# Weight chunks laid out by the host as they lie in SBUF: one run per partition in place of 1 KB pieces

## The chip, the cores and the metric

The kernel runs on one core of a Trainium2 chip. The metric is the device time of one execution in microseconds (us); the times below are of whole executions, the profile is of one execution taken by the hardware profiler. TensorE (PE) does the matmuls, VectorE (DVE) and ScalarE (ACT) the work on elements, GpSimd (POOL) a little at the end of a layer; SyncE (SP) only issues DMAs. The DMA engines copy between the chip's main memory (HBM) and the 128 partitions of the on-chip memory (SBUF).

## The reference

A generator of two layers over 256 latent and 256 context tokens of width 1024. Layer 0 works on all 512 tokens, layer 1 needs an output for the 256 latent ones only. Cut to what matters:

```python
def trunk_layer(x, xc, mod, mod_c, ...):
    sh1, sc1, g1, sh2, sc2, g2 = split(mod, 6)           # mod = silu(c) @ w_ada + b_ada
    h = modulate(rms_norm(x, norm1), sh1, sc1)           # the same for the context: hc
    y, yc = token_mixer(h, hc, ...)
    x = x + g1 * y
    x = x + g2 * moe_ffn(modulate(rms_norm(x, norm2), sh2, sc2), ...)

def token_mixer(h, hc, ...):
    f_in, p_in, qb, kb, vb, qw, kw, vw = split(h @ w_in)
    # a: Fourier mix of f_in, b: global attention, c: window attention, d: pooling of p_in
    return branch_merge(h, (out_a, out_b, out_c, out_d), w_branch, w_gate, b_gate, w_out)

def branch_merge(h, branches, w_branch, w_gate, b_gate, w_out):
    merged = zeros_like(h)
    for i, br in enumerate(branches):
        gate = sigmoid(h @ w_gate[i] + b_gate[i])
        merged = merged + gate * (br @ w_branch[i])
    return merged @ w_out

def moe_ffn(h, router_w, router_bias, w1, w3, w2):       # 16 experts of width 512, 2 per token
    for e in range(N_EXPERTS):
        hid = silu(tok @ w1[e]) * (tok @ w3[e])
        out = out + combine[:, e:e + 1] * (hid @ w2[e])
```

All weights are float32, and nearly all of the time goes with reading them: 2 layers with 16 experts of 6 MB, 24 MB of w_ada, 16 MB of w_gate, 8 MB of w_branch, 4 MB of w_out and some 10 MB of w_in.

## The kernel before

**Weights come in chunks.** A chunk is at most 1 MB and lies in SBUF as 128 partitions of 2048 float32 (CH = 2048, 8 KB). The class `Stream` keeps the chunks in the order of their use, which a dry run of the whole program takes down. `fill` issues loads on SyncE's queue as far as the rings have room: `stage` has four buffers; while the experts run there is also the ring `ext`, and some large tiles (`hH`, `hL`, `X`) serve as buffers when nothing else is in them. `load` issues a chunk's DMA. `emit` (called from `tick` and `get`) splits a chunk into a high and a low float16 part: `whi` on ScalarE (L325) and then `wlo` on VectorE (L329). Three matmuls (`mm3`, L586 to L588) put a product together from the parts: `hH` by `whi`, `hL` by `whi`, `hH` by `wlo`. The chunks of w_ada are used in float32 as they come (L506).

**The kinds of chunks** are in `load`. `cols` (w_in, w_gate, w_out, w1, w3) and `ada` take 256 columns of a matrix of 1024 rows: row p + 128 k goes to partition p, so that a partition gets eight pieces of 1 KB, from eight rows. `half` takes 128 columns, eight pieces of 512 bytes. `rows` takes `n` columns of a matrix of 512 rows, four pieces a partition: 1 KB for w_branch (n = 256), 2 KB for w2 (n = 512, also as `raw`). `q` takes 256 columns out of 512, in two DMAs of 512-byte pieces. `heads` (w_branch of branches b and c) has rows by head and takes two DMAs, one for partitions 0 to 63 and one for 64 to 127, each 256 KB.

**The order of work.** A scheduler sets the order of every engine's instructions ahead of time; each engine then runs its own list in order, and SyncE's list is one queue of DMAs. The transposes of the attention probabilities (`pt` or `pair` from `P`, L778) go through the same queue of SyncE. The tiles of x and ctx, the tables, and the experts' results go through ScalarE's queue.

**The places that matter here.** At the start `ada` (L502 on) turns the conditioning vectors into shifts and scales (`adah`, `adal`, L483 and L484), while ScalarE sums the squares of x (L536). `gated(i)` (L1002 on) runs four steps for each of the four branches; a step takes a w_gate chunk, makes two `gate` tiles on ScalarE (L1019), takes a w_branch chunk and adds the product to `merged`. The `po` matmuls (L846) of attention read the transposed `pt`. Each of 16 experts takes two chunks of w1, two of w3 and two of w2; `sa` (L1393) on ScalarE is reached once an expert, `hd` are its hidden values. In the trace w1, w2 and w3 have one name, `in_w_dram`. During `gated` of branch c the first expert chunks are already being loaded into `ext`.

Of the kernel before, what the change touches and what calls it, by code (L numbers as in the profile page):

```python
# [19 lines left out]
KD = D // 128  # L20
T = 256
NTOK = 512
HD = 64
# [6 lines left out]
WS = 512.0  # L30
# [83 lines left out]
class Dry:  # L114
    """Stands in for the chip while the order of the weight chunks is taken down."""

# [19 lines left out]
class Pool:  # L136
    def __init__(self, pool, bufs):
        self.pool, self.bufs = pool, bufs
# [6 lines left out]
def k8(t):  # L145
    return t.rearrange("p (k c) -> p k c", k=KD)


def k4(t):
    return t.rearrange("p (k c) -> p k c", k=4)  # L150


class Stream:
    """Weight chunks in the order of their use: DMAs run ahead as far as staging space goes, and
    each chunk's fp16 high and low parts are made up to `look` chunks ahead."""

# [38 lines left out]
    def load(self, spec, st):  # L195
        A, sp = self.kn.A, self.kn.nc.sync
        if self.behind:
            self.kn.tc.keep_in_program_order(self.kn.nc.vector.memset(st.rearrange("p (k c) -> p k c", c=128)[:, :, 0:1], 0.0))
        kind, name, idx, c0 = spec[:4]
        w = A[name]  # L200
        for i in idx:
            w = w[i]
        if kind == "half":
            sp.dma_start(k8(st[:, 0:1024]), w[:, c0:c0 + 128].rearrange("(k p) c -> p k c", p=128))
        elif kind in ("cols", "ada"):
            sp.dma_start(k8(st), w[:, c0:c0 + 256].rearrange("(k p) c -> p k c", p=128))
        elif kind == "q":
            src = w[:, c0:c0 + 512].rearrange("(k p) (a c) -> p k a c", p=128, a=2)[:, :, :, spec[4] * 128:spec[4] * 128 + 128]
            view = st.rearrange("p (k a c) -> p k a c", k=KD, a=2)
            for a in range(2):  # L210
                sp.dma_start(view[:, :, a, :], src[:, :, a, :])
        elif kind in ("rows", "raw"):
            n = spec[4]
            sp.dma_start(k4(st[:, 0:4 * n]), w[:, c0:c0 + n].rearrange("(k p) c -> p k c", p=128))
        else:
            n = spec[4]
            src = w[:, c0:c0 + n].rearrange("(a j d) n -> a d j n", a=2, j=4)
            for a in range(2):
                sp.dma_start(k4(st[a * HD:(a + 1) * HD, 0:4 * n]), src[a])

# [17 lines left out]
    def emit(self, j):  # L238
        spec, st = self.order[j], self.stage[j]
        if self.piece == 0:  # L240
            pool = self.kn.wsp
            if self.kn.ext is not None and spec[1] in ("w1", "w2", "w3"):
                self.parts += 1
                if self.parts % (NWSP + self.kn.more) < self.kn.more:
                    pool = self.kn.ext
            self.tiles[j] = tuple(pool.tile([128, CH], F16, name=n) for n in ("whi", "wlo"))
        hi, lo = self.tiles[j]
        if spec[0] == "q":
            u = self.piece
            d = lambda t: t.rearrange("p (k u a d) -> p k u a d", k=KD, u=2, a=2)[:, :, u]  # L250
            src = st.rearrange("p (k a u d) -> p k a u d", k=KD, a=2, u=2)[:, :, :, u]
            self.kn.split(d(hi), d(lo), src, WS)
            done = u == 1
        else:
            n = 1024 if spec[0] == "half" else 4 * spec[4] if spec[0] in ("rows", "heads") else CH
            step = CH if spec[1] in ("w1", "w2", "w3") else 1024
            s = slice(self.piece * step, min(n, (self.piece + 1) * step))
            self.kn.split(hi[:, s], lo[:, s], st[:, s], WS)
            done = (self.piece + 1) * step >= n
        self.piece += 1  # L260
        if done:
            self.piece = 0
            self.split += 1
            self.stage.pop(j)
# [50 lines left out]
class Kernel:  # L315
    def __init__(self, tc, A, out, orders, dry=False):
        self.tc, self.A, self.out, self.orders, self.dry = tc, A, out, orders, dry
        self.nc = tc.nc
        self.ext = None
        self.h_free = False  # L320
        self.pin = False
# [17 lines left out]

# [1 line left out]
    def setup(self, ctx):  # L341
# [48 lines left out]
    def table_load(self, lo, hi):  # L390
        """Part of the staged constants, asked for once the vector engine has come this far."""
        st = self.wk.tile([128, 512], F32, "tabs", tag="t2")
        self.after(self.nc.vector.memset(st[:, 0:1], 0.0))
        self.nc.scalar.dma_start(st[:, 0:hi - lo], self.A["staged"][:, lo:hi])
        return st
# [70 lines left out]

# [1 line left out]
    def ada(self, l, which, tick=True):  # L468
# [63 lines left out]

# [1 line left out]
    def x_stat(self, t, part, lo, n):  # L534
# [54 lines left out]

# [1 line left out]
    def layer(self, l):  # L591
# [492 lines left out]

# [1 line left out]
    def moe(self, l, nt, side):  # L1086
# [172 lines left out]
        def experts(W, hot0, h2):  # L1259
# [35 lines left out]
            def slot_side(e):  # L1295
                """The weights of the expert's slots and its one-hot turned to slots by tokens."""
                g, el = divmod(e, EPG)
# [132 lines left out]
            def side_rows():  # L1430
                """Room and rows that the end needs, once the last group is dispatched."""
                m = self.lay.tile([128, KD, nt], F32, "merged").rearrange("p k c -> p (k c)")
# [92 lines left out]

_RAW = ["x", "ctx", "w_ada", "w_in", "sink", "pool_w", "w_branch", "w_gate", "w_out",
        "router_w", "router_bias", "w1", "w3", "w2", "norm_f"]


def host_arrays(inputs):  # L1530
    arr = {n: np.ascontiguousarray(inputs[n]) for n in _RAW}
# [7 lines left out]
    feature = np.r_[1:64, 0, 64, 127:64:-1]  # L1539
    w = arr["w_branch"]  # L1540
    order = np.r_[tuple(g * 128 + feature for g in range(4))]
    arr["w_branch"] = np.ascontiguousarray(np.concatenate([w[:, 0:1, order], w[:, 1:]], 1))
    arr["consts"], arr["staged"] = shape_constants()
    return arr


def build(inputs):
    import concourse.bacc as _bacc

    nc = _bacc.Bacc("TRN2", target_bir_lowering=False, num_devices=1)  # L1550
    arrays, A = {}, {}
    for name, a in host_arrays(inputs).items():
        arrays[f"in_{name}_dram"] = a
        A[name] = nc.dram_tensor(f"in_{name}_dram", a.shape, mybir.dt.from_np(a.dtype), kind="ExternalInput").ap()
    out = nc.dram_tensor("out_0_dram", (1, T, D), F32, kind="ExternalOutput").ap()
    orders = {}
    Kernel(Dry(), Dry(), Dry(), orders, dry=True).body()
    with tile.TileContext(nc) as tc:
        Kernel(tc, A, out, orders).body()
    return nc, arrays  # L1560
# [8 lines left out]
```

## Time and profile before

| | us |
|---|---|
| three runs | 1497.1, 1509.64, 1510.03 |
| median | 1509.64 |
| span of the profiled execution | 1507.6 |
| TensorE busy | 1389.0 (92%) |
| VectorE busy | 1122.6 (74%) |
| ScalarE busy | 954.0 (63%) |
| SyncE's DMA queue, time with packets, share of the span | 78.8% |
| TensorE waiting for the first w_ada chunk | 12.06 |
| ScalarE's `whi` waiting for expert chunks, whole run | 25.0 |
| `po` waiting for transposes `pt`, whole run | 11.2 |

The profile of the execution lists no time besides its span, which is 2.0 us below the median of the runs. A busy share is an average over the whole program; stretches differ, so the rows further below are taken by stage. An engine's wait is put down to the event that came last.

### The profile page before, as it was taken

The numbers are of one execution on the slowest core, as the hardware profiler recorded it, in microseconds if no ns is written. First come the engines' busy times: TensorE is split into PE (matmuls) and PEld (weight loads), VectorE is DVE, ScalarE is ACT, GpSimd is POOL, SyncE is SP. The second block draws the span as 40 slices with busy tenths as digits, with TensorE's granted clock in tenths as the row PEclk, the third lists the DMA queues.
The fourth block names the chain that finished last, engine by engine and source line by source line (L and its number), as shares of the span: only waits on it lengthen the run. The fifth ranks groups of instructions, "written<-read, shape, count | busy, mean of one in ns | idle before, by whom it ended". The sixth has DMA issues, their size and how long they took to land. (4 is left out here: it accounts for less than half of the span.)

```text
span 1507.6 us, 33938 instructions
## 1 busy us (share of the span) xinstructions
PE 1389.0 (92%) x14303; PEld 941.7 (62%) x14303; DVE 1122.6 (74%) x2039; ACT 954.0 (63%) x1437; POOL 8.8 (1%) x12
## 2 busy tenths in 40 slices
PE   4999999997999998999999878899798889999995
PEld 2545454443444686777777556687686767777773
DVE  3888548767435576898968778869856788988797
ACT  3767535655223457898887466747645578787783
POOL 0000000000000000000000200000000000000000
PEclk9999999998999999999999989999999999999998
DMA  9759864898696346999999873976989879999980
GB/s 331 227 134 221 226 189 114 197 225 219 202 281 199 128 141 235 337 342 365 366 367 361 284 226 120 227 183 164 224 211 299 293 250 325 359 357 362 351 299 31
DMA packets 403194, 375.83 MB, mean 249 GB/s; under 512 B 91728, under 2 KB 364112, under 8 KB 402768
## 3 DMA queue, kind: packets, MB, share of 16 engines
q1 hardware_dynamic: 393616, 355.24, 78.8%
q10 hardware_dynamic: 8256, 14.05, 2.6%
q0 software_dynamic: 1152, 4.19, 0.8%
q8 instruction: 116, 1.90, 0.5%
q14 instruction: 54, 0.44, 0.1%
HBM read 342.78 MB, written 9.70 MB: 234 GB/s over the span
## 5 line engine op out<-in xcount | busy, mean ns | idle before, releaser
L586 PE MATMUL mm<-hH,whi 128*128 128x96 f16 (+2 forms) x1824 | 400.6, 262 | 6.1 <-ACT gate L1019 5.4
L588 PE MATMUL mm<-hH,wlo 128*128 128x96 f16 (+2 forms) x1824 | 400.1, 262 | 4.4 <-DVE wlo L329 4.4
L587 PE MATMUL mm<-hL,whi 128*128 128x96 f16 (+2 forms) x1824 | 400.3, 262 | 0.0
L329 DVE SCALAR_TENSOR_TENSOR wlo<-stage,whi 128x1024 f16<-128x1024 f32 (+1 forms) x208 | 310.3, 1506 | 112.2 <-ACT whi L325 111.3
L586 PEld LDWEIGHTS <-whi 128*128 128x128 f16 x3104 | 305.3, 98 | 79.4 <-issue 6.0
L588 PEld LDWEIGHTS <-wlo 128*128 128x128 f16 x3104 | 305.2, 98 | 78.9 <-DVE wlo L329 6.7
L587 PEld LDWEIGHTS <-whi 128*128 128x128 f16 x3104 | 305.3, 98 | 77.4 <-issue 5.4
L325 ACT ACTIVATE whi<-stage 128x1024 f16<-128x1024 f32 (+1 forms) x208 | 262.2, 1282 | 124.6 <-PE mm L587 77.4
L329 DVE SCALAR_TENSOR_TENSOR wlo<-ext,whi 128x2048 f16<-128x2048 f32 x116 | 262.7, 2285 | 75.3 <-ACT whi L325 75.3
L325 ACT ACTIVATE whi<-ext 128x2048 f16<-128x2048 f32 x116 | 218.7, 1905 | 52.3 <-DMA ext<-in_w_dram 25.0
L586 PE MATMUL mm<-xg,whi 128*128 128x96 f16 x1024 | 132.5, 206 | 0.0
L588 PE MATMUL mm<-xg,wlo 128*128 128x96 f16 x1024 | 132.5, 206 | 0.0
L587 PE MATMUL mm<-xg,whi 128*128 128x96 f16 x1024 | 132.5, 206 | 0.0
L587 PE MATMUL py<-wlo,hd 128*96 128x512 f16 x224 | 84.9, 379 | 4.3 <-DVE wlo L329 4.2
L588 PE MATMUL py<-whi,hd 128*96 128x512 f16 x224 | 84.7, 381 | 2.8 <-DVE hd L327 2.3
L586 PE MATMUL py<-whi,hd 128*96 128x512 f16 x224 | 85.1, 380 | 1.7 <-ACT hd L325 1.7
L586 PE MATMUL mm<-brH,whi 128*128 128x512 f16 (+1 forms) x256 | 83.5, 326 | 0.0
L587 PE MATMUL mm<-brL,whi 128*128 128x512 f16 (+1 forms) x256 | 83.4, 326 | 0.0
L588 PE MATMUL mm<-brH,wlo 128*128 128x512 f16 (+1 forms) x256 | 83.4, 326 | 0.0
L1277 PE MATMUL mm<-Dg,merged 128*128 128x384 f16 x384 | 75.7, 340 | 5.2 <-ACT hH L1279 2.6
L506 PE MATMUL mm<-stage,cpad 128*32 128x256 f32 x768 | 58.1, 406 | 16.0 <-DMA stage<-in_w_ada_dram 16.0
L830 ACT ACTIVATE P<-E,rl 128x512 f16<-128x512 f32 (+1 forms) x96 | 57.1, 643 | 13.2 <-issue 4.9
(311 smaller groups left out, 2128.4 us busy)
## 6 DMA issues: line engine op xcount, KB each, us to landing
ext<-in_w_dram SPq DMA_DIRECT2D x118, 1024.0 KB, 11.5
stage<-in_w_dram SPq DMA_DIRECT2D x62, 1024.0 KB, 10.2
stage<-in_w_ada_dram SPq DMA_DIRECT2D x48, 1024.0 KB, 6.7
stage<-in_w_gate_dram SPq DMA_DIRECT2D x32, 1024.0 KB, 6.0
stage<-in_w_in_dram SPq DMA_DIRECT2D x24, 512.0 KB, 6.4
stage<-in_w_in_dram SPq DMA_DIRECT2D x8, 1024.0 KB, 7.2
stage<-in_w_branch_dram SPq DMA_DIRECT2D x16, 512.0 KB, 4.5
stage<-in_w_branch_dram SPq DMA_DIRECT2D x32, 256.0 KB, 6.6
```

What stands on the lines that cost most here:

```text
L325: a = nc.scalar.activation(hi, src, AF.Copy, scale=scale)
L329: b = nc.vector.scalar_tensor_tensor(lo, src, scale, hi, op0=ALU.mult, op1=ALU.subtract)
L506: pe.matmul(ps[32 * j:32 * j + 32, :], self.cpad[:, 2 * k:2 * k + 32], st[:, k, :], start=k < 4, stop=k >= 4, tile_position=(0, 32 * j))
L586: pe.matmul(ps, wH(k), xH(k), start=first and k == 0, stop=False)
L587: pe.matmul(ps, wH(k), xL(k), start=False, stop=False)
L588: pe.matmul(ps, wL(k), xH(k), start=False, stop=last and k == nk - 1)
L830: act.activation(pv[:, 0, qt, :], E[qt][:, 0:nk], AF.Copy, scale=r[:, qt:qt + 1])
L1277: pe.matmul(ps[:, 0:SLOTS], h2[n][t][:, cs(k)], Dg[:, t].rearrange("p e c -> p (e c)"), start=t == 0, stop=t == ntt - 1)
```

## The change

The host now cuts every weight chunk out of its matrix and writes it as it will lie in SBUF, [128, 2048] float32, all chunks of one weight stacked in one array: a partition's share is one run of 8 KB (4 KB for `half` and w_branch). To know the chunks, the dry run is made ahead of the host's arrays. `load` is then the same single DMA for every kind, `q` and `heads` included; the eight pieces, the two DMAs of `q` and the two of `heads` are gone. `q` lies so that its two halves, which are split one at a time, are contiguous columns. The number of bytes, the rings and the matmuls are the same.

```diff
+def chunk_width(spec):
+    return 1024 if spec[0] == "half" else 4 * spec[4] if spec[0] in ("rows", "raw", "heads") else CH
+
+
+def chunk_of(spec, w):
+
+    kind, _, idx, c0 = spec[:4]
+    for i in idx:
+        w = w[i]
+    n = {"half": 128, "cols": 256, "ada": 256, "q": 512}.get(kind) or spec[4]
+    w = w[:, c0:c0 + n]
+    if kind == "q":
+        w = w.reshape(KD, 128, 2, 2, 2, HD)[:, :, :, spec[4]]
+        return w.transpose(1, 0, 3, 2, 4).reshape(128, CH)
+    if kind == "heads":
+        return w.reshape(2, 4, HD, n).transpose(0, 2, 1, 3).reshape(128, 4 * n)
+    return w.reshape(-1, 128, n).transpose(1, 0, 2).reshape(128, -1)
...
-        kind, name, idx, c0 = spec[:4]
-        w = A[name]
-        for i in idx:
-            w = w[i]
-        if kind == "half":
-            sp.dma_start(k8(st[:, 0:1024]), w[:, c0:c0 + 128].rearrange("(k p) c -> p k c", p=128))
-        elif kind in ("cols", "ada"):
-            sp.dma_start(k8(st), w[:, c0:c0 + 256].rearrange("(k p) c -> p k c", p=128))
-        elif kind == "q":
-            src = w[:, c0:c0 + 512].rearrange("(k p) (a c) -> p k a c", p=128, a=2)[:, :, :, spec[4] * 128:spec[4] * 128 + 128]
-            view = st.rearrange("p (k a c) -> p k a c", k=KD, a=2)
-            for a in range(2):
-                sp.dma_start(view[:, :, a, :], src[:, :, a, :])
-        elif kind in ("rows", "raw"):
-            n = spec[4]
-            sp.dma_start(k4(st[:, 0:4 * n]), w[:, c0:c0 + n].rearrange("(k p) c -> p k c", p=128))
-        else:
-            n = spec[4]
-            src = w[:, c0:c0 + n].rearrange("(a j d) n -> a d j n", a=2, j=4)
-            for a in range(2):
-                sp.dma_start(k4(st[a * HD:(a + 1) * HD, 0:4 * n]), src[a])
+        n = chunk_width(spec)
+        sp.dma_start(st[:, 0:n], A[spec[1]][self.kn.places[spec[1:]]][:, 0:n])
...
-        if spec[0] == "q":
-            u = self.piece
-            d = lambda t: t.rearrange("p (k u a d) -> p k u a d", k=KD, u=2, a=2)[:, :, u]
-            src = st.rearrange("p (k a u d) -> p k a u d", k=KD, a=2, u=2)[:, :, :, u]
-            self.kn.split(d(hi), d(lo), src, WS)
-            done = u == 1
-        else:
-            n = 1024 if spec[0] == "half" else 4 * spec[4] if spec[0] in ("rows", "heads") else CH
-            step = CH if spec[1] in ("w1", "w2", "w3") else 1024
-            s = slice(self.piece * step, min(n, (self.piece + 1) * step))
-            self.kn.split(hi[:, s], lo[:, s], st[:, s], WS)
-            done = (self.piece + 1) * step >= n
+        n = chunk_width(spec)
+        step = CH if spec[1] in ("w1", "w2", "w3") else 1024
+        s = slice(self.piece * step, min(n, (self.piece + 1) * step))
+        self.kn.split(hi[:, s], lo[:, s], st[:, s], WS)
+        done = (self.piece + 1) * step >= n
...
+    chunks, places = {}, {}
+    for specs in orders.values():
+        for spec in specs:
+            if spec[1:] not in places:
+                at = chunks.setdefault(spec[1], [])
+                places[spec[1:]] = len(at)
+                at.append(chunk_of(spec, w_branch if spec[1] == "w_branch" else np.asarray(inputs[spec[1]])))
+    for name, at in chunks.items():
+        arr[name] = np.stack([np.pad(c, ((0, 0), (0, max(x.shape[1] for x in at) - c.shape[1]))) for c in at])
```

The order of TensorE's and GpSimd's instructions is the same in both kernels. The scheduler, which counts one DMA where there were two, has moved a few rows on the other engines. The largest such place is `gated` of branch c in layer 1. On SyncE's queue it reads, before (`ext` are the experts' chunks that are loaded ahead, `stage` those of the gates and branches, and the numbers tell one buffer from another):

```order
L206 DMA stage_19520<-in_w_gate_dram 128x8x256
L206 DMA ext_20227<-in_w3_dram 128x8x256
L219 DMA stage_19556<-in_w_branch_dram 64x4x256 x2
L206 DMA stage_19619<-in_w_gate_dram 128x8x256
L219 DMA stage_19655<-in_w_branch_dram 64x4x256 x2
L206 DMA ext_20229<-in_w3_dram 128x8x256
L206 DMA stage_19718<-in_w_gate_dram 128x8x256
```

and after:

```order
L219 DMA ext_20203<-in_w3_dram 128x2048
L219 DMA stage_19499<-in_w_gate_dram 128x2048
L219 DMA stage_19535<-in_w_branch_dram 128x1024
L219 DMA ext_20205<-in_w3_dram 128x2048
L219 DMA stage_19597<-in_w_gate_dram 128x2048
L219 DMA stage_19633<-in_w_branch_dram 128x1024
```

The first w3 chunk now stands ahead of a gate chunk that it stood behind, and the second (ext_20229 before, ext_20205 after) ahead of the next gate and branch chunks. On ScalarE the same stretch reads, before (a `gate` is made from the product of the gate's chunk, a `whi` is the high part of a chunk):

```order
L1019 ACTIVATE gate<-mm,hbg 128x256
L325 ACTIVATE whi<-stage 128x1024 x2
L1019 ACTIVATE gate<-mm,hbg 128x256
L325 ACTIVATE whi<-stage 128x1024
L1019 ACTIVATE gate<-mm,hbg 128x256
L325 ACTIVATE whi<-ext 128x2048
L325 ACTIVATE whi<-stage 128x1024 x2
L325 ACTIVATE mH_20051<-merged 128x256
```

and after:

```order
L1013 ACTIVATE gate<-mm,hbg 128x256
L319 ACTIVATE whi<-ext 128x2048
L319 ACTIVATE whi<-stage 128x1024 x2
L1013 ACTIVATE gate<-mm,hbg 128x256
L319 ACTIVATE whi<-stage 128x1024
L1013 ACTIVATE gate<-mm,hbg 128x256
```

The split of that w3 chunk has moved four places up, ahead of two gates and the splits between them. The corresponding split in layer 0 has moved two places up, ahead of one gate and one split, and one transpose in attention of layer 0 has changed places with a gate chunk's load.

## Rows read from the trace of the kernel before

**Rows 1.** The page's parts 1 to 3: busy engines, packets, SyncE's queue (q1).

```profile
PE 1389.0 (92%) x14303; PEld 941.7 (62%) x14303; DVE 1122.6 (74%) x2039; ACT 954.0 (63%) x1437; POOL 8.8 (1%) x12
DMA packets 403194, 375.83 MB, mean 249 GB/s; under 512 B 91728, under 2 KB 364112, under 8 KB 402768
q1 hardware_dynamic: 393616, 355.24, 78.8%
```

**Rows 2.** Windows: us; PE, PEld, DVE, ACT, POOL busy; PE clock, DMA share, GB/s.

```profile
700.00:750.00 50.00, 48.61 (x769) 39.65 (x768) 46.97 (x31) 42.83 (x38) 0.00 (x0) 1.00 1.08 365
800.00:825.00 25.00, 21.24 (x316) 16.58 (x313) 22.19 (x14) 18.40 (x15) 0.00 (x0) 1.00 1.07 358
1300.00:1350.00 50.00, 49.49 (x660) 36.74 (x657) 42.80 (x35) 44.80 (x48) 0.00 (x0) 1.00 1.07 359
```

**Rows 3.** Timeline of ScalarE, experts of layer 0: start, duration, instruction, wait.

```profile
728.14 0.48 ACT L1393 ACTIVATE sa<-mm 128x384 f32<-128x384 f32 x1
741.46 0.47 ACT L1393 ACTIVATE sa<-mm 128x384 f32<-128x384 f32 x1
...
797.74 0.48 ACT L1393 ACTIVATE sa<-mm 128x384 f32<-128x384 f32 x1
814.50 0.49 ACT L1393 ACTIVATE sa<-mm 128x384 f32<-128x384 f32 x1 [0.21 <-ACT whi L325]
823.96 1.91 ACT L325 ACTIVATE whi<-stage 128x2048 f16<-128x2048 f32 x1 [1.33 <-DMA stage<-in_w_dram]
831.44 0.47 ACT L1393 ACTIVATE sa<-mm 128x384 f32<-128x384 f32 x1
```

**Rows 4.** Layer 1, 1100 to 1150: SyncE's and ScalarE's timeline; waits (total, times, longest).

```profile
1124.85 1.17 SPq L206 DMA_DIRECT2D ext<-in_w_dram  x1
1139.86 1.91 ACT L325 ACTIVATE whi<-ext 128x2048 f16<-128x2048 f32 x1 [9.12 <-DMA ext<-in_w_dram]
PE mm L586 <- ACT gate L1019: 5.4, 1, 5.4
```

**Rows 5.** DMA from 1100 to 1150: packets; issues (KB each, us to landing).

```profile
DMA packets 12557, 12.63 MB, mean 253 GB/s; under 512 B 288, under 2 KB 12552, under 8 KB 12552
stage<-in_w_branch_dram SPq DMA_DIRECT2D x8, 256.0 KB, 11.7
```

**Rows 6.** Windows behind two pauses of TensorE, columns as in rows 2.

```profile
1087.00:1096.00 9.00, 8.97 (x62) 6.98 (x62) 0.48 (x1) 0.95 (x2) 0.00 (x0) 0.69 0.35 112
1145.00:1154.00 9.00, 8.71 (x57) 6.80 (x58) 7.62 (x13) 5.10 (x9) 0.00 (x0) 0.69 1.09 318
```

**Rows 7.** Waits of the whole run, and SyncE's timeline around the longest transpose wait.

```profile
PE po L846 <- DMA pt<-P: 11.2, 4, 6.6
ACT whi L325 <- DMA stage<-in_w_gate_dram: 10.5, 8, 2.9
1077.00 1.00 SPq L206 DMA_DIRECT2D stage<-in_w_gate_dram  x1
1079.28 0.37 SPq L214 DMA_DIRECT2D stage<-in_w_branch_dram  x1
```

**Rows 8.** DMA of the start: 11 to 30 us, then 6 to 9.5 with ScalarE's queue (q10).

```profile
DMA packets 6801, 6.59 MB, mean 347 GB/s; under 512 B 421, under 2 KB 6671, under 8 KB 6799
DMA packets 599, 1.40 MB, mean 400 GB/s; under 512 B 32, under 2 KB 332, under 8 KB 599
q10 hardware_dynamic: 299, 1.09, 79.6%
```

**Rows 9.** VectorE's split of expert chunks, by form: count, busy, mean ns, idle before.

```profile
L329 DVE SCALAR_TENSOR_TENSOR wlo<-ext,whi 128x2048 f16<-128x2048 f32 x116 | 262.7, 2285 | 75.3 <-ACT whi L325 75.3
```

**Rows 10.** Timelines at the start: first matmul, last x tile, VectorE's first constant.

```profile
12.06 1.93 PE L506 MATMUL mm<-stage,cpad 128*32 128x256 f32 x16 [12.06 <-DMA stage<-in_w_ada_dram]
11.08 0.63 ACT L536 ACTIVATE junk<-X 128x512 f32<-128x512 f32 x1 [0.46 <-DMA X<-in_ctx_dram]
22.03 0.23 DVE L377 CAST id<-cst 128x128 f16<-128x128 f32 x1 [7.12 <-DMA cst<-in_consts_dram]
```

More of the change, by code (lines that the diff above doesn't have):

```diff
@@ L315, with __init__ @@
 class Kernel:
-    def __init__(self, tc, A, out, orders, dry=False):
+    def __init__(self, tc, A, out, orders, places=None, dry=False):
+        self.places = places if places is not None else Dry()
         self.tc, self.A, self.out, self.orders, self.dry = tc, A, out, orders, dry
@@ L1523, in moe, with host_arrays @@
         self.moe_scope.close()
-_RAW = ["x", "ctx", "w_ada", "w_in", "sink", "pool_w", "w_branch", "w_gate", "w_out",
-        "router_w", "router_bias", "w1", "w3", "w2", "norm_f"]
-def host_arrays(inputs):
+_RAW = ["x", "ctx", "sink", "pool_w", "router_w", "router_bias", "norm_f"]
+def host_arrays(inputs, orders):
     arr = {n: np.ascontiguousarray(inputs[n]) for n in _RAW}
@@ L1539, in host_arrays @@
     feature = np.r_[1:64, 0, 64, 127:64:-1]
-    w = arr["w_branch"]
+    w = np.asarray(inputs["w_branch"])
     order = np.r_[tuple(g * 128 + feature for g in range(4))]
-    arr["w_branch"] = np.ascontiguousarray(np.concatenate([w[:, 0:1, order], w[:, 1:]], 1))
+    w_branch = np.concatenate([w[:, 0:1, order], w[:, 1:]], 1)
     arr["consts"], arr["staged"] = shape_constants()
-    return arr
+    chunks, places = {}, {}
[7 more added lines that the diff above has]
+        arr[name] = np.stack([np.pad(c, ((0, 0), (0, max(x.shape[1] for x in at) - c.shape[1]))) for c in at])
+    return arr, places
 def build(inputs):
@@ L1550, in build @@
     nc = _bacc.Bacc("TRN2", target_bir_lowering=False, num_devices=1)
+    orders = {}
+    Kernel(Dry(), Dry(), Dry(), orders, dry=True).body()
     arrays, A = {}, {}
-    for name, a in host_arrays(inputs).items():
+    arr, places = host_arrays(inputs, orders)
+    for name, a in arr.items():
         arrays[f"in_{name}_dram"] = a
@@ L1555, in build @@
     out = nc.dram_tensor("out_0_dram", (1, T, D), F32, kind="ExternalOutput").ap()
-    orders = {}
-    Kernel(Dry(), Dry(), Dry(), orders, dry=True).body()
     with tile.TileContext(nc) as tc:
-        Kernel(tc, A, out, orders).body()
+        Kernel(tc, A, out, orders, places).body()
     return nc, arrays
```

## The prediction

> **What bounds the kernel now.** I began with the page's totals [rows 1]. TensorE is busy for 1389.0 of 1507.6 us, so all that shorter weight transfers can give lies in the other 118.6 us, less those that are chains between the engines, and in stretches at the lower clock. The queue that SyncE feeds has packets under way for 78.8% of the span; most packets are under 2 KB. So transfers are nearly always running; the question is where the program waits for them. That was read stage by stage.
>
> First the 50 us windows of the experts [rows 2]. In layer 0 from 700 to 750 the transfer engines are never idle, and bring 365 GB/s; still TensorE works 48.61 of 50 us, since the staging rings were full when the experts began. From 800 to 825 it is only 21.24 of 25: the rings have run dry. The pace of the experts says it again [rows 3]: from one `sa` to the next it is 741.46 - 728.14 = 13.32 us while fed, but 16.76 us from 797.74 to 814.50 and 16.94 us from there to 831.44, and in that stretch `whi` waits for its chunk (1.33 us at 823.96). In layer 1, between 1300 and 1350, the transfers run as hard (359 GB/s) but TensorE works 49.49 of 50 us: there nothing is to be won.
>
> Second the sums of waits and the places they point to. The longest stall of TensorE on a chunk after the start is in layer 1's `gated(2)` [rows 4]: a matmul waits 5.4 us for `gate` on ScalarE; ScalarE stood 9.12 us before `whi<-ext` at 1139.86, and that chunk had been issued at 1124.85. In those 50 us the engines move only 253 GB/s [rows 5]: the `heads` pieces go to 64 partitions a time, and a 256 KB transfer takes 11.7 us from issue to landing, behind others of its kind. A pause of TensorE costs twice: the 9 us after it ran at a mean granted clock of 0.69 [rows 6], the lower of the two levels (1.2 and 2.4 GHz) for most of them. Third, transposed attention probabilities travel on the same queue: `po` waits 11.2 us in four places for `pt` [rows 7], the longest 6.6, and the 9 us after that show 0.69 too [rows 6].
>
> **The change, part by part.** The same bytes move, in the same order but for a few swaps, in one piece per partition. I need the rate for large pieces. The nearest rows are of the start [rows 8]. From 11 to 30 us, when nearly all packets are under 2 KB, 347 GB/s; from 6 to 9.5 us, when half of the packets are the 4 KB rows of x and ctx (299 packets with 1.09 MB), 400 GB/s. With every weight packet at 4 or 8 KB I take 400 GB/s; the bounds are the 365 of [rows 2] (no gain) and some 420, an estimate that carries the step from 347 to 400, which came with half of the packets, a little further. A loss is a rival below.
>
> One rule speaks against this change. The row first: 400 GB/s with large pieces, for 3.5 us, against 347 to 365 without [rows 2, 8]. The Trainium skill, "DMA: Bandwidth & Descriptors", section "Where 436 GB/s comes from", says that for transfers between HBM and SBUF the memory's share per core, about 358 GB/s, is what binds; the trace goes above it, if briefly and alone. By the rule the sum below would keep only what is won in layer 1's `gated(2)`.
>
> *Experts of layer 0.* An expert takes six chunks, 6.29 MB: 17.2 us at 365 GB/s, 15.7 us at 400. All 96 chunks of a layer, 100.7 MB, take 275.8 us at 365 and 251.7 at 400. The last of them would be there 24 us earlier, and the dry rings cost only some 7 us (below); so any rate over about 375 GB/s (7 us in 276) is enough, and the exact one doesn't matter. What is late next is VectorE: six `wlo` of 2285 ns [rows 9], with the two steps on `sa` and `hd` about 14.8 us for an expert. If the starved two go at the fed pace, 16.76 + 16.94 - 2 x 13.32 = 7.1 us are won; at VectorE's, 16.76 + 16.94 - 2 x 14.8 = 4.1. I take **5**, as VectorE enters the stretch with some lead.
>
> *Layer 1's gated(2).* The `heads` chunks fill 128 partitions in one DMA. At 350 to 400 GB/s in place of 253, the queue in front of the `ext` chunk is gone sooner: in the 15.0 us from issue to landing it moved 3.8 MB, which take 9.5 us at 400. That is 5.5 us sooner, which alone covers the 5.4 us of stall; besides, SyncE issues this load a slot earlier, ahead of a gate chunk of 1 MB (2.6 us at 400). ScalarE's `whi<-ext` also stands four places earlier in its queue, ahead of two gates, so that if the chunk were still late it would hold up more than before. I take the stall as gone, 5.4 us (bounds 2 and 5.4), and with it the low clock behind it: (1 - 0.69) x 9 = 2.8 us. Together **8.2** (5 to 8.2). In layer 0 the same place has no stall of TensorE, and its moved rows are costed at nothing: by the code each matmul there takes 512 tokens in place of 256, which leaves twice the time.
>
> *Transposes.* Ahead of the worst `pt` lie a gate chunk and a branch chunk, 1.57 MB [rows 7]: 4.3 us at 365 GB/s, 3.9 at 400, so each of the four waits is cut by 0.4 us, 1.6 in all, taken as **2**. The bounds are the longest wait, 6.6 us, with the clock's 2.8 us on top, if the queue is free when the transpose is issued, and 0.
>
> *Gate chunks.* `whi` waits 10.5 us for them in eight places [rows 7]; little of it reaches TensorE, which has matmuls of the gate before. **1** (0 to 3).
>
> *Start.* The first matmul waits 12.06 us for its first chunk, since the x tiles come at the same time over ScalarE's queue; of the 599 packets between 6 and 9.5 us, 299 belong to that queue [rows 8], so the rest, nearly as many, to SyncE's: one for one. If that holds for packets of 8 KB beside 4 KB, the 512 rows of x share with 4.2 MB of weights, not 0.5 MB: the last x tile comes about 9 us later (3.7 MB at 400), at about 20 in place of 11.08 us [rows 10], while the chunks come that much earlier. The square sums then end at about 21.5, just about when VectorE's `id<-cst` (22.03) lets the steps behind it go. **0**, from 3 won (chunks are no longer late after that) to 5 lost (x late).
>
> *The rest.* `q` in one DMA, its split in contiguous halves, SyncE with 24 issues less (8 for `q`, 16 for `heads`): SyncE is no bound, and `q` is split beside matmuls: 0, if the cover goes 1 or 2 us. The swapped rows in attention of layer 0: 0 (-2 to 2).
>
> The sum is 5 + 8.2 + 2 + 1 = 16.2 us off the span of 1507.6, 1491.4. The profile has no time of its own besides this span; the median of the three runs is 2.0 above it, so I forecast **1493**. A change of under 1% (15.1 us) can't well be told from none here; faster by over 1% begins at 1494.5.
>
> **Rivals.**
>
> *The rate does not rise* (365 GB/s stays, what binds is not the piece). For it: three stretches, 700 to 750, 1300 to 1350 and 11 to 30, lie within 347 to 365 although the mix of pieces differs. Against it: the 400 of [rows 8], short as it is. Then the experts, the transposes and the gates keep their times, and only the 64 partitions are mended: 1507.6 - 8.2 + 2 = 1501. The rule quoted above gives this result.
>
> *Every wait on a transfer goes, and the clock stays high.* 7.1 for the experts, 8.2, 9.4 for the transposes, 3 for the gates, 3 at the start: 30.7, so 1507.6 - 30.7 + 2 = 1479. For it: the queue gets faster for all of these at once, and a pause that ends sooner also saves the clock. Against it: most of these waits end on VectorE or ScalarE shortly after, which get no faster.
>
> *Slower: large pieces come at a lower rate.* Each transfer engine now reads 8 KB from one place at a time. The place is the experts of layer 0, which draw all that comes; it decides as soon as the rate falls below 365. At 335, a loss of about the size of the gain that I assume, the 96 chunks need 300.5 us, 24.7 more; layer 1, whose queue is just as full but not waited for, some 12 more; with 8 us won in `gated(2)` that is 1507.6 + 24.7 + 12 - 8 + 2 = 1538. Against it: the rows of x are pieces of 4 KB and came fast.
>
> **How the numbers follow.** The forecast has 0.47: its own range is 1487 to 1500, of which about two thirds (0.30) lie below 1494.5. No rise of the rate 0.26, about 1501. All waits gone 0.20. Slower 0.07. So faster 0.30 + 0.20 = 0.50, same 0.17 + 0.26 = 0.43, slower 0.07. The range runs from 1475, beyond the sum of the upper bounds by some us, to 1508, the end of the second case with 5 us lost at the start and the swapped rows on top; it leaves out the slower rival and the outermost of the others.
>
> **What would show it.** Right: over 375 GB/s in layer 0's experts from 650 on, no fall of TensorE's share in the last 50 us of them, and `sa` to `sa` below 15 us throughout; no stall above 2 us in layer 1's `gated(2)` and a clock of 1.00 behind it; the median landing of `w_branch` near half of what it was. Wrong: the same GB/s at full queues; or a new wait of ScalarE for `ext` ahead of the gates; or x that lands so late that the first norm waits for it beyond 24 us; or a queue that is faster, and the same pace of experts, with VectorE busy all through.

## The result, and the profile after

The changed kernel takes 1484.4 us, median of four runs (1481.73 to 1486.71); the kernel before 1507.36 (1497.1 to 1510.03). The ratio is 0.9856, with a 95% interval of 0.9819 to 0.9893: 16 to 27 us faster. The forecast was 1493 in a range of 1475 to 1508, so the sign and the range held, and the gain between the medians, 23 us, was larger by some 7 us than the sum.

The page of the kernel after, lines of its head and of its parts 1 to 3, which answer to [rows 1]:

```profile
span 1480.0 us, 33882 instructions
PE 1378.1 (93%) x14303; PEld 938.7 (63%) x14303; DVE 1122.7 (76%) x2039; ACT 954.3 (64%) x1437; POOL 8.6 (1%) x12
DMA packets 142713, 375.82 MB, mean 254 GB/s; under 512 B 91344, under 2 KB 93392, under 8 KB 104400
q1 hardware_dynamic: 133136, 355.24, 68.5%
```

The span is 27.6 us shorter, more than the 23 us between the medians: the span of 1507.6 belongs to one of the longer runs of the kernel before, that of 1480.0 to the shortest of the four of the kernel after. TensorE's work is the same; 10.9 us of the difference are busy time (1389.0 to 1378.1, the same matmuls at a higher mean clock) and 16.7 idle time. The same 355.24 MB of SyncE's queue go in a third of the packets, and its packets are under way for 68.5% of a shorter span, not 78.8%. The windows of layer 0's experts (columns as in [rows 2]):

```profile
650.00:700.00 50.00, 48.52 (x656) 36.87 (x653) 45.69 (x27) 44.34 (x46) 0.00 (x0) 1.00 1.01 417
700.00:750.00 50.00, 48.82 (x765) 39.51 (x763) 46.98 (x30) 44.32 (x38) 0.00 (x0) 1.00 1.00 400
800.00:825.00 25.00, 23.27 (x353) 18.44 (x352) 24.53 (x13) 22.04 (x18) 0.00 (x0) 1.00 0.93 382
```

417 and 400 GB/s stand where 365 did, and from 800 to 825 TensorE works 23.27 of 25 us in place of 21.24. The timeline of ScalarE there, which answers to [rows 3], has no wait on a chunk:

```profile
793.79 0.48 ACT L1387 ACTIVATE sa<-mm 128x384 f32<-128x384 f32 x1
807.11 0.47 ACT L1387 ACTIVATE sa<-mm 128x384 f32<-128x384 f32 x1
822.73 0.48 ACT L1387 ACTIVATE sa<-mm 128x384 f32<-128x384 f32 x1
834.42 0.47 ACT L1387 ACTIVATE sa<-mm 128x384 f32<-128x384 f32 x1
```

The steps from `sa` to `sa` are 13.32, 15.62 and 11.69 us; before, the first two were 16.76 and 16.94. VectorE, and TensorE's waits from 804 to 823, show what sets the second step now:

```profile
799.27 11.09 DVE L323 SCALAR_TENSOR_TENSOR wlo<-ext,whi 128x2048 f16<-128x2048 f32 x5
810.28 0.55 DVE L1388 SCALAR_TENSOR_TENSOR sa<-mm,sa 128x384 f32<-128x384 f32 x1
810.75 4.49 DVE L323 SCALAR_TENSOR_TENSOR wlo<-ext,whi 128x2048 f16<-128x2048 f32 x2
815.15 0.55 DVE L321 TENSOR_TENSOR hd<-sa,hd 128x384 f16<-128x384 f32 x1
815.62 4.49 DVE L323 SCALAR_TENSOR_TENSOR wlo<-stage,whi 128x2048 f16<-128x2048 f32 x2
```

```profile
PEld L582 <- DVE hd L321: 2.3, 1, 2.3
PE py L581 <- DVE wlo L323: 1.6, 1, 1.6
```

VectorE works without a pause from 799.27 to 820.11, and TensorE (PEld is its weight load) waits for VectorE's `hd` and `wlo`, no longer for chunks. For layer 1's `gated(2)`, ScalarE's timeline (to [rows 4]), the transfers of 1080 to 1130 (to [rows 5]) and windows (to [rows 6]) follow:

```profile
1107.51 1.91 ACT L319 ACTIVATE whi<-ext 128x2048 f16<-128x2048 f32 x1 [1.38 <-DMA ext<-in_w_dram]
```

```profile
stage<-in_w_branch_dram SPq DMA_DIRECT2D x5, 512.0 KB, 4.5
```

```profile
1080.00:1130.00 50.00, 50.00 (x464) 44.52 (x463) 34.42 (x49) 28.00 (x38) 0.00 (x0) 1.00 0.88 339
1123.00:1132.00 9.00, 9.00 (x85) 8.07 (x83) 6.75 (x13) 5.55 (x9) 0.00 (x0) 1.00 1.01 413
1071.00:1080.00 9.00, 9.00 (x61) 6.92 (x61) 1.02 (x3) 1.36 (x3) 0.00 (x0) 0.67 0.33 118
```

TensorE is busy for all of the 50 us at 339 GB/s, its clock stays at 1.00 behind the place, a branch chunk of 512 KB lands 4.5 us after its issue where 256 KB took 11.7, and ScalarE waits 1.38 us for the chunk, not 9.12. The low clock behind the long wait for a transpose (0.67) is still there.

**Where the time went.** TensorE's list of 14303 matmuls is the same in every kernel of this study but the one with transposes on ScalarE's queue, where it differs in places of the attention; so the same matmul can be found in two traces and its start compared. The table gives, for stretches that end at the matmuls which start at the times of the first row in the kernel before, by how many us each kernel is shorter (-) or longer than that trace; the first two kernels are second profiles of before and after, described with the experiments.

| stretch ends (us) | 40 | 400 | 600 | 860 | 1080 | 1120 | 1160 | 1220 | 1493 |
|---|---|---|---|---|---|---|---|---|---|
| before, again | 0.8 | -0.9 | 2.0 | -0.1 | 0.5 | -0.4 | -2.2 | -3.1 | 0.0 |
| after, again | -1.4 | -2.1 | 0.1 | -7.2 | -0.7 | -0.3 | -8.8 | -3.0 | 0.0 |
| after | -1.9 | -2.3 | 2.1 | -8.9 | -3.7 | -1.2 | -8.8 | -3.1 | 0.0 |
| heads alone | 0.5 | -1.4 | 2.1 | 0.9 | -0.7 | 0.0 | -8.7 | -3.3 | 0.0 |
| experts alone | 0.3 | 1.0 | 0.0 | -9.0 | -1.2 | -0.1 | -8.0 | -1.8 | 0.0 |
| heads by halves | -1.5 | 0.4 | 0.0 | -9.0 | -1.9 | 0.3 | -8.2 | -1.7 | 0.0 |
| heads by columns | -1.9 | -2.2 | 2.0 | -8.6 | -3.9 | -1.0 | -8.8 | -3.3 | 0.0 |
| 1 KB pieces | 1.1 | -1.2 | 0.2 | 6.2 | 0.2 | 0.3 | -8.0 | -2.0 | 0.0 |
| 2 KB pieces | 0.4 | -1.7 | 0.2 | -7.3 | 0.1 | -0.4 | -8.8 | -1.7 | 0.0 |
| 4 KB pieces | -1.0 | -2.4 | 0.2 | -7.3 | -3.0 | -0.7 | -8.8 | -3.3 | 0.0 |
| x ahead | -3.1 | -3.0 | 0.0 | -8.7 | -2.4 | -1.6 | -8.8 | -1.9 | 0.0 |

Two columns carry the gain: layer 0's experts (600 to 860) and layer 1's `gated(2)` (1120 to 1160).

### The profile page after: what moved, and what is told of

Its sections match the earlier page's. It is cut to its first block, busy times and chain, and to the rows that moved or that the text cites. A ratio compares the mean times of both kernels' runs of the same rounds, so it can differ in the third digit from the quotient of the medians.

```text
span 1480.0 us, 33882 instructions
## 1 busy us (share of the span) xinstructions
PE 1378.1 (93%) x14303; PEld 938.7 (63%) x14303; DVE 1122.7 (76%) x2039; ACT 954.3 (64%) x1437; POOL 8.6 (1%) x12
## 3 DMA queue, kind: packets, MB, share of 16 engines
q1 hardware_dynamic: 133136, 355.24, 68.5%
## 5 line engine op out<-in xcount | busy, mean ns | idle before, releaser
L580 PE MATMUL mm<-hH,whi 128*128 128x96 f16 (+2 forms) x1824 | 396.5, 260 | 0.7 <-DVE gate L998 0.7
L581 PE MATMUL mm<-hL,whi 128*128 128x96 f16 (+2 forms) x1824 | 396.3, 260 | 0.0
L500 PE MATMUL mm<-stage,cpad 128*32 128x256 f32 x768 | 58.5, 408 | 12.4 <-DMA stage<-in_w_ada_dram 12.3
L825 DVE SCALAR_TENSOR_TENSOR P<-E,rl,P 128x512 f16<-128x512 f32 (+1 forms) x96 | 59.2, 659 | 7.7 <-ACT P L824 7.6
```

The costliest lines, as they stand in the source:

```text
L500: pe.matmul(ps[32 * j:32 * j + 32, :], self.cpad[:, 2 * k:2 * k + 32], st[:, k, :], start=k < 4, stop=k >= 4, tile_position=(0, 32 * j))
L580: pe.matmul(ps, wH(k), xH(k), start=first and k == 0, stop=False)
L581: pe.matmul(ps, wH(k), xL(k), start=False, stop=False)
L825: dve.scalar_tensor_tensor(pv[:, 1, qt, :], E[qt][:, 0:nk], r[:, qt:qt + 1], pv[:, 0, qt, :], op0=ALU.mult, op1=ALU.subtract)
```

## The experiments

**Heads alone.** The kernel before, in which only the `heads` chunks of w_branch are laid out by the host; their place in `load`:

```diff
+def whole_run(spec):
+    return spec[0] == "heads"
...
+        if whole_run(spec):
+            n = chunk_width(spec)
+            sp.dma_start(st[:, 0:n], A["run_" + spec[1]][self.kn.places[spec[1:]]][:, 0:n])
+            return
```

> The kernel before, with the heads chunks of w_branch alone laid out as one run of 4 KB in 128 partitions, one DMA each; all other chunks keep their 1 KB pieces. The order in gated(2) of layer 1 is that of the kernel after (the w3 chunk's load a slot earlier, its split four places up). If the 64 partitions and the order made the stall there: the 5.4 us are gone or nearly, the 50 us around it move over 320 GB/s in place of 253, and some 8 us come off (about 1500 us); the experts of layer 0 keep 365 GB/s and their 16.8 us starved pace. If the stall was there because of 1 KB pieces: it stays over 3 us, and the time stays within 3 us of before.

Measured: 1498.47 us, ratio 0.9948 (0.9931 to 0.9965). The stall is gone, 8.7 us less in that column, and the experts are as before (365 GB/s). The first reading held: the 1 KB pieces of the other chunks do not make the stall by themselves. The run changes three things of the `heads` chunks at once, the 64 partitions, their pieces (4 KB in place of 1) and the moved rows, and doesn't tell these apart. Its transfers of 1100 to 1150, to be set beside [rows 5], and ScalarE's wait:

```profile
DMA packets 14264, 16.48 MB, mean 330 GB/s; under 512 B 284, under 2 KB 13235, under 8 KB 14259
```

```profile
1126.88 1.91 ACT L353 ACTIVATE whi<-ext 128x2048 f16<-128x2048 f32 x1 [3.55 <-DMA ext<-in_w_dram]
```

330 GB/s stand where 253 did, as expected (over 320). ScalarE still waits 3.55 us for the chunk, and TensorE has work meanwhile.

**Experts alone.** The kernel before, with `whole_run` true for w1, w3 and w2 only. Not a row of ScalarE's order is moved.

> The kernel before, with the chunks of w1, w3 and w2 alone as one run of 8 KB a partition; gates, branches, w_in, w_out and w_ada as before, and ScalarE's order is that of before in every row. If the sum of the parts holds: the experts of layer 0 win 7 to 9 us, with about 400 GB/s from 650 on; the stall in layer 1's gated(2) stays at 4 to 6 us since the heads pieces are the same; the start is unchanged; about 1499 us. If the gains are not separate (the experts' chunks already stand in the queue of gated(2)): the stall shrinks too, by more than 2 us.

Measured: 1489.12 us, ratio 0.9894 (0.9846 to 0.9941). The experts win 9.0 us at 414 and 400 GB/s, as expected; but the stall in `gated(2)` is gone as well (8.0 us), with `heads` by halves, their 1 KB pieces and the old order. So the parts don't add, and the second reading held: the two runs alone are 7.5 and 16.9 us faster than the kernel before, 24.4 together, while the whole change gives 23.0 and, in its second set of runs, 17.1. The DMA issues from 1090 to 1140 (KB each, us to landing), then the timelines of SyncE and ScalarE:

```profile
ext<-in_run_w_dram SPq DMA_DIRECT2D x6, 1024.0 KB, 10.4
stage<-in_w_branch_dram SPq DMA_DIRECT2D x8, 256.0 KB, 8.5
```

```profile
1115.30 0.60 SPq L224 DMA_DIRECT2D ext<-in_run_w_dram  x1
1125.55 1.91 ACT L353 ACTIVATE whi<-ext 128x2048 f16<-128x2048 f32 x1 [4.62 <-DMA ext<-in_run_w_dram]
```

The chunk starts to be split 10.25 us after its issue, where it took 15.01 before; ScalarE's wait shrinks from 9.12 to 4.62 us, and these 4.5 us are enough for TensorE to wait no more. Large `ext` chunks alone, or whole `heads` (with the moved rows) alone, each take the stall away.

**Heads by halves.** The kernel after, with two DMAs for a `heads` chunk, 64 partitions each:

```diff
+        src = A[spec[1]][self.kn.places[spec[1:]]]
+        if spec[0] == "heads":
+            for a in range(2):
+                sp.dma_start(st[a * HD:(a + 1) * HD, 0:n], src[a * HD:(a + 1) * HD, 0:n])
...
```

> The kernel after, but each heads chunk comes by two DMAs of 64 partitions (runs of 4 KB); everything else is 8 KB runs. The scheduler returns the rows of gated(2) to the order of before. If half the partitions move at half the rate whatever the size of a run, and that is what makes the stall: the branch chunks keep their slow landing, under 300 GB/s around 1100 to 1150, and a stall of 2 to 5 us with a low clock behind it is back, 1488 to 1493 us. If the size of the runs was the cause: no stall, within 2 us of the kernel after (1484).

Measured: 1487.02 us, ratio 0.9885 (0.9843 to 0.9927). The stretch of 1090 to 1140 moves 301 GB/s, and a half takes 8.8 us to land. The slow halves are real: from 1095 to 1125 a packet of 4 KB takes 323 ns on average, where it takes 170 from 1085 to 1125 in the kernel after, to 128 partitions. But no stall is left (8.2 us won): ScalarE waits 4.4 us for the chunk, again below what TensorE notices. My reading that the halves would bring it back fell; the time is 2.6 us above the kernel after, and the two intervals overlap.

**Heads by columns.** The same with two DMAs of 512 columns on all partitions.

> The kernel after, but each heads chunk comes by two DMAs of 512 columns, over all 128 partitions (runs of 2 KB). The order in gated(2) is that of before, as in the run with halves. If the order (the load a slot later, the split behind the gates) makes the stall: 2 to 5 us of stall as with the halves. If it is the 64 partitions: no stall over 1 us, within 2 us of the kernel after.

Measured: 1483.36 us, ratio 0.9855 (0.982 to 0.989), as the kernel after. The DMA issues from 1090 to 1140, first with halves, then with columns:

```profile
stage<-in_w_branch_dram SPq DMA_DIRECT2D x8, 256.0 KB, 8.8
stage<-in_w_branch_dram SPq DMA_DIRECT2D x8, 256.0 KB, 5.7
```

Two DMAs for a chunk, in smaller pieces but on all partitions, land sooner, so the slow landing comes with the 64 partitions and not with the second DMA. One premise of the expectation was wrong: the scheduler left the rows of `gated(2)` in the order of the kernel after, so this run says nothing about the order. The order of before is free of the stall in the two runs before it (experts alone, heads by halves); whether the moved rows alone, with halves of 1 KB pieces, would remove it wasn't tried.

**Size of the pieces.** The kernel after with its order unchanged; the host lays a chunk as planes, so that a partition's 8 KB are pieces of PIECE columns of float32:

```diff
+PIECE = 256
...
+        src = A[spec[1]][self.kn.places[spec[1:]]].rearrange("k p c -> p k c")
+        sp.dma_start(st[:, 0:n].rearrange("p (k c) -> p k c", c=PIECE), src[:, 0:n // PIECE])
...
+        arr[name] = np.ascontiguousarray(wide.reshape(len(at), 128, -1, PIECE).transpose(0, 2, 1, 3))
```

PIECE is 256 for pieces of 1 KB, 512 and 1024 for 2 and 4 KB; `wide` holds the chunks as the kernel after has them.

> The kernel after with every row of its order the same, but a partition's 8 KB are eight pieces of 1 KB from eight planes of 128 KB (the host lays each chunk as planes). If the size of a piece sets the rate: 350 to 370 GB/s in layer 0's experts, the rings run dry again near 800, and the experts give back 7 to 9 us, while the stall in gated(2) stays away; about 1493 us. If the scatter of pieces over far rows of the matrix was what held the rate: near 400 GB/s and 1484 us.

> The kernel after, order unchanged, pieces of 2 KB from four planes. With a fixed time for each piece the rate lies between those of 1 KB and 8 KB, nearer to 8 KB: about 385 GB/s in layer 0's experts, which is above the 375 that they need, so the experts' pace stays under 15 us. If the gain came only with the largest pieces: 365 GB/s, dry rings.

> The kernel after, order unchanged, pieces of 4 KB from two planes. If the cost is a fixed time for each piece: over 390 GB/s in layer 0's experts and no loss in time against the kernel after. If a partition's whole chunk must be one run: a rate clearly below, 380 or less, and dry rings.

Measured: 1507.55 us with 1 KB, ratio 1.0007 (0.9985 to 1.0028); one run each of 1490.23 with 2 KB and 1483.23 with 4 KB. Windows of layer 0's experts with 1, then 2, then 4 KB:

```profile
700.00:750.00 50.00, 48.16 (x765) 39.14 (x764) 45.33 (x29) 41.17 (x37) 0.00 (x0) 1.00 1.09 354
750.00:800.00 50.00, 45.12 (x545) 32.77 (x543) 34.09 (x20) 38.85 (x44) 0.00 (x0) 0.93 1.09 352
```

```profile
700.00:750.00 50.00, 48.66 (x770) 39.68 (x769) 46.97 (x31) 44.34 (x39) 0.00 (x0) 1.00 1.05 389
```

```profile
700.00:750.00 50.00, 48.66 (x745) 39.06 (x742) 46.97 (x29) 44.92 (x39) 0.00 (x0) 1.00 1.03 404
```

With 1 KB the rings are dry as early as 750 to 800: TensorE works 45.12 of 50 us there, at 0.93 of its clock. The rate follows the size: 354, 389, 404 and, with 8 KB, 417 (650 to 700; the 400 of 700 to 750 has a dip to 236 GB/s in it, in which the transfer engines were not always busy). With 1 KB it is no better out of planes, where neighbouring partitions' pieces lie side by side, than out of the matrix's far rows; it is a little worse than the 365 of before, in which w2 had pieces of 2 KB, and the experts lose 6.2 us by it. So the gain of the experts is the size alone, and the layout without it gives nothing. From 2 KB on the experts' column is -7.2 to -9.0 whatever the size: 389 GB/s are enough, as the 375 of the prediction said. The stall in `gated(2)` is gone even with 1 KB pieces (8.0 us), at 354 GB/s, by whole `heads` and the moved rows. The expected 1493 was missed: with 1 KB the experts take 15 us more than in the kernel after, not 7 to 9.

**x ahead.** The kernel after, in which x, ctx and the first constants go on SyncE's queue ahead of the w_ada chunks:

```diff
+        head = CONST_AT["slot"][0]
+        self.load_x(sp)
+        sp.dma_start(self.cst[:, 0:head], A["consts"][:, 0:head])
         self.W = Stream(self, 0, 2)
         if not self.dry:
             self.W.fill()
-        head = CONST_AT["slot"][0]
-        sp.dma_start(self.cst[:, 0:head], A["consts"][:, 0:head])
-        self.load_x(act)
```

> The kernel after, with the loads of x, ctx and the first constants issued on SyncE's queue ahead of the first w_ada chunks, in place of ScalarE's queue beside them. In the kernel after the last x tile lands at 16.4 us, the chain from it ends at 20.2, and the first step behind it on TensorE is at 20.54. If x had become the bound of the start: x lands by 9, and that first step comes at 17.5 to 19, so 1.5 to 3 us off, with the rest unchanged. If the w_ada chunks, which then come later, are the bound: the first matmul moves from 8.8 to about 11, the third chunk ends at 17 or later, and nothing or a loss of up to 1 us results.

Measured: 1482.69 us, ratio 0.9852 (0.9812 to 0.9892), not to be told from the kernel after by its time. By the trace the start is 1.2 us shorter than after's (-3.1 against -1.9), less than the 1.5 to 3 expected of the first reading; x lands at 11.65, not by 9, and the first matmul starts at 14.39, not at about 11. First the kernel before, then the kernel after, then this one, by the timelines of ScalarE, TensorE and VectorE:

```profile
22.39 0.16 PE L483 MATMUL mm<-sel,adah 128*128 128x2 f16 x1 [1.72 <-DVE sel L377]
```

```profile
16.43 0.63 ACT L530 ACTIVATE junk<-X 128x512 f32<-128x512 f32 x1 [2.48 <-DMA X<-in_ctx_dram]
8.78 1.93 PE L500 MATMUL mm<-stage,cpad 128*32 128x256 f32 x16 [8.78 <-DMA stage<-in_w_ada_dram]
20.54 0.16 PE L477 MATMUL mm<-sel,adah 128*128 128x2 f16 x1 [2.39 <-DVE sel L371]
20.11 0.16 DVE L459 SCALAR_TENSOR_TENSOR rnorm<-rs_t,rs_y 128x1 f32<-128x1 f32 x1
```

```profile
11.65 0.63 ACT L530 ACTIVATE junk<-X 128x512 f32<-128x512 f32 x1 [0.44 <-DMA X<-in_ctx_dram]
14.39 1.93 PE L500 MATMUL mm<-stage,cpad 128*32 128x256 f32 x16 [14.39 <-DMA stage<-in_w_ada_dram]
19.26 1.07 PE L500 MATMUL mm<-stage,cpad 128*32 128x256 f32 x16 [1.00 <-DMA stage<-in_w_ada_dram]
20.27 0.18 PE L477 MATMUL mm<-sel,adah 128*128 128x2 f16 x1
```

The step at 22.39 stood behind the constants before (22.03 in [rows 10]). In the kernel after x is the last to come (16.43), and the chain from it on VectorE ends just before the step at 20.54; with x ahead it is there at 11.65, and the third w_ada chunk, which starts at 19.26, holds the step at 20.27. The bound changes hands between two transfers; only what comes after it is earlier.

**Transposes on ScalarE's queue.** The kernel with x ahead, and one word changed:

```diff
-                        nc.sync.dma_start_transpose(out=o, in_=i)
+                        nc.scalar.dma_start_transpose(out=o, in_=i)
```

> The kernel with x ahead, and besides the transposes of attention issued on ScalarE's queue in place of SyncE's, so that they no longer stand behind the weights. In the kernel after `po` still waits 10.3 us for `pt` in five places, the longest 5.3. If the wait is the queue in front: most of it goes, 5 to 9 us off, up to 3 more by the clock: 1472 to 1478. If a transpose takes its 4 to 5 us by itself, or ScalarE, which then spends the issue time (up to 4 us each on SyncE) in its own row, becomes the bound of attention: no gain, or slower, 1485 to 1500, with new waits for `P`, `E` and `gate` in attention of both layers.

Measured: 1542.24 us, ratio 1.0268 (1.0227 to 1.0309). Attention of layer 0 is 28 us longer than with x ahead, that of layer 1 some 29. The transposes in its tile view, the same in the kernel after, and the waits of this run:

```profile
L772 ACTq DMA_TRANSPOSE pt<-P x16: 1333/1964/9114, 950.8 to 1120.5; - x16
DMA to landing us min/median/max: 4.3/4.9/16.8
```

```profile
L772 SPq DMA_TRANSPOSE pt<-P x16: 1318/3320/4950, 925.3 to 1065.9; - x16
DMA to landing us min/median/max: 4.3/5.5/7.8
```

```profile
PE po L840 <- DMA pt<-P: 19.5, 8, 5.3
PE po L840 <- DMA pair<-P: 15.1, 6, 4.8
```

Off the queue of the weights a transpose still takes 4.3 us at least and 4.9 in the middle, where it took 4.3 and 5.5 on SyncE's queue, and its issue blocks ScalarE's list for 1.96 us in the middle, up to 9.1. The second reading held, with a loss beyond the 1500 that it allowed: most of the wait for `pt` is not the queue in front, and SyncE's queue is the better place for the transposes. The weights still move beside them here; how long a transpose takes with no other transfer wasn't measured.

**Both kernels again.** A second profile of after and of before, word for word the same.

> The kernel after once more, word for word, for a second profile. If the differences in the stretches without weight waits (540 to 600, 900 to 965 and 1160 to 1220 us of the kernel before, where the traces differ by 2 to 3 us at another granted clock) belong to the change: they are the same again to some tenths. If the clock there differs from one execution to the next: one or more of them come out otherwise by 1 us or more.

> The kernel before once more, word for word, for a second profile: the 5.4 us stall in layer 1's gated(2) and the starved experts of layer 0 (16.8 us) must be there again, to some tenths, if they belong to the kernel; the stretches without weight waits show how far two executions of one kernel differ there.

Measured: after 1486.08 us, ratio 0.9877 (0.9849 to 0.9905); before 1505.97, one run. The starved experts of before are there again. The stall in `gated(2)` is there too, with one microsecond less:

```profile
PE mm L586 <- ACT gate L1019: 4.3, 1, 4.3
```

But the stretches without weight waits differ between two executions of one kernel: 540 to 600 costs the second profile of before 2.0 us more and 1160 to 1220 gives it 3.1, where the second of after has 0.1 and -3.0. The granted clock differs with them: from 540 to 600 it is 0.97 in the first profile of before and 0.91 in the second, from 1150 to 1220 0.90 and 0.95. So the 3.1 us after 1160 that the first pair of traces seems to show is not the change's. Likewise after's -3.7 before 1080 is only -0.7 in its second profile. The spans of the two second profiles lie 19.9 us apart, those of the first two 27.6.

## Why the prediction was right, and where its sizes were not

*Experts of layer 0.* Forecast 5; the first pair of profiles shows 8.9 and the second 7.1 (7.2 against the first profile of before). For the two steps that the sum was made of, the forecast came true: 16.76 + 16.94 became 13.32 + 15.62, 4.8 us less. As forecast, one goes at the fed pace and the other is held by VectorE, which in the window of 800 to 825 works 24.53 of 25 us. In the second profile of after that step takes 17.21 us, at a mean granted clock of 0.91 from 805 to 823 in place of 1.00, that is, in part at the lower of the clock's two levels (it takes 17.18 in the runs with 2 and 4 KB pieces as well), so that the two steps win 3.0 against the second profile of before (16.42 and 17.06). What the sum left out are two more steps that waited for chunks. Before:

```profile
746.51 1.91 ACT L325 ACTIVATE whi<-ext 128x2048 f16<-128x2048 f32 x1 [0.56 <-DMA ext<-in_w_dram]
749.52 1.91 ACT L325 ACTIVATE whi<-ext 128x2048 f16<-128x2048 f32 x1 [1.10 <-DMA ext<-in_w_dram]
762.33 0.48 ACT L1393 ACTIVATE sa<-mm 128x384 f32<-128x384 f32 x1
844.84 0.48 ACT L1393 ACTIVATE sa<-mm 128x384 f32<-128x384 f32 x1
```

and after:

```profile
739.38 0.48 ACT L1387 ACTIVATE sa<-mm 128x384 f32<-128x384 f32 x1
758.38 0.48 ACT L1387 ACTIVATE sa<-mm 128x384 f32<-128x384 f32 x1
```

The step from 741.46 to 762.33 loses 1.9 us (20.87 to 19.00), the one from 831.44 to 844.84 loses 1.7 (13.40 to 11.69); with 0.6 behind the last `sa` that makes the 8.9. So the 7.1 was a bound for two steps and not for the stretch. The sign "below 15 us throughout" failed, in part because it was badly chosen: fed steps of 19.00 and 20.63 us stand in the kernel after as well; 13.32 was the shortest step of its group. The other signs of being right are there: the rate, TensorE's share at the end of the experts, the landing of the branch chunks, and the clock of 1.00 behind `gated(2)`.

*Rate.* Taken as 400, measured 417 and 400; the rival without a rise of the rate is excluded: the lower of the two is above 365, and the runs with 1, 2 and 4 KB show the rate rising with the size. The Trainium skill's sentence of 358 GB/s ("DMA: Bandwidth & Descriptors", "Where 436 GB/s comes from") doesn't hold here: 400 to 417 GB/s for 50 us at a time on one core.

*Layer 1's gated(2).* Forecast 8.2; 8.8 against the first profile of before, 6.6 against the second. The mechanism is shown, the time of the `ext` chunk in the queue: from its issue to the start of its split it is 15.01 us before, 7.94 after, 10.10 with heads alone, 10.25 with experts alone, 10.19 with halves and 10.75 with 1 KB pieces, and none of these five stalls. So there is more than one way to shorten it. Of the causes, large `ext` chunks are shown to be enough by themselves (experts alone); whole `heads` are shown to be enough only together with the moved rows (heads alone, 1 KB pieces). The new place of `whi<-ext` ahead of two gates, which I feared, costs nothing: the chunk is there 1.38 us after ScalarE asks for it, and TensorE doesn't wait.

*Transposes.* Forecast 2, of it seen: the wait for `pt` goes from 11.2 to 10.3 us, 11.3 and 11.1 in the second profiles, and the longest from 6.6 to 5.3, 6.2 and 6.1. So it is nearer to 1, or the lower bound of 0; the run on ScalarE's queue shows why: the transpose's own 4 to 5 us are most of each wait, not the chunks ahead of it.

*Gate chunks.* Forecast 1; `whi` waits 12.3 and 13.1 us for them in the two profiles of after, 10.5 and 14.0 in those of before: nothing.

*Start.* Forecast 0; 1.9 and 1.4 us won, 2.7 and 2.2 against the second profile of before. That x comes later was right; its time was not (16.43, not the 20 that I worked out), and behind its last sum of squares the chain on VectorE up to `rnorm`, which ends at 20.27, was not counted. What the term had wrong are the constants: they held the step at 22.39 before, and I left them at 22.03; after, VectorE doesn't wait for them, and the step follows x's chain, 1.85 us sooner. Beyond the sum lie the 40 to 400 us: -2.3 and -2.1 where the second profile of before has -0.9; their cause stays open.

*The sum.* 16.2 was forecast; the spans show 27.6 and, with the second profiles, 19.9. Two terms, transposes and gate chunks (3 together), hardly came, and the experts, the start and the 40 to 400 us brought more than they were given. That the sum comes as near as it does is in part luck. The measured 1484.4 is nearer to the 1479 of the rival in which every wait goes than to 1493, but the rival's transposes and gate chunks (12.4 of its 30.7 us) did not come either.

*Slower* needed large pieces to come at under 365 GB/s; no size from 2 KB up did.

## What to carry to other kernels

Where transfers are always under way and an engine waits for them, the size of the contiguous piece is worth having from 2 KB on, and a new order in memory without larger pieces gives nothing. A stall that several causes share goes when any of them does, so its price belongs to no single one and must not be added up by parts. Waits on a transfer have to be counted through the whole stretch and not only where they are longest, here four steps and not two; and a stretch whose clock changes must be profiled twice before its difference is put down to a change.

## What I had not expected of the hardware

From the four rates, 16 engines need for one piece 16 x 1024 / 354 = 46 ns at 1 KB, 84 at 2 KB (389 GB/s), 162 at 4 KB (404) and 314 at 8 KB (417): some 38 to 39 ns for each KB and about 8 ns for each piece, an estimate that takes the engines as never idle. The Trainium skill, "DMA: Bandwidth & Descriptors", section "Why small descriptors are slow (HBM only)", has a fixed 3 cycles for each packet beside one cycle for 32 bytes: by it 1 KB pieces would come at (32 / 35) / (256 / 259) = 92.5% of the rate of 8 KB, an estimate; the section's 32 bytes of descriptor for each operation, counted as one cycle more, make it 90.3%. Measured are 354 / 417 = 85%, so small pieces cost more here.

A piece that goes to 64 partitions takes nearly twice as long: 323 ns for 4 KB in the run with halves, 170 ns in the kernel after, to 128 partitions.

Two executions of the kernel before differ by 2.0 us in one stretch with short pauses of TensorE and by 3.1 in another, in opposite directions. That is as much as several terms of the sum.
